# A hybrid mLSTM and attention block on one core: weight blocks split two ahead, and the end of a head in three steps

## Chip, core and metric

The kernel runs on one core of a Trainium2 chip. The metric is the device time of one execution in microseconds (us). The engines are named as in the profile: PE is TensorE, PEld its weight loads, DVE is VectorE, ACT is ScalarE, POOL is GpSimd, SP is SyncE, which here issues most of the DMAs.

## What is computed

One layer over 256 latent tokens and 256 context tokens of width 2048, all in float32. Cut to what matters here:

```python
p   = u @ w_in                       # u: normalised, modulated tokens
h   = mlstm_chunked(q, k, v, ...)    # 8 heads, both directions, dv = 256
h   = rms_norm(h_f + h_b)            # per head
y_a = (sigmoid(o_a) * h * silu(z_a)) @ w_branch_a
y_b = (attention(q_b, k_b, v_b) * silu(z_b)) @ w_branch_b
out = (sigmoid(g_a) * y_a + sigmoid(g_b) * y_b) @ w_out
x   = layer_norm(ALPHA * x + gate * out)
```

o_a, z_a, q_b, z_b, g_a and g_b are columns of p.

## The kernel before

Every large product is made of three matmuls: each float32 operand is split into a high half (rounded to the matmul's float32r) and a low half (what the rounding left), and high x high, high x low and low x high are added up (`three`, lines 335 to 338, and `three_b`, 340 to 343). A weight matrix is read in blocks of 512 KB (`raw`, three buffers, loaded by SP, `fetch_ahead`, line 308). A block is split by two instructions (`split`, 330): ACT casts `raw` to `whi`, then DVE subtracts and writes `wlo`. Two pairs of `whi` and `wlo` lie in one pool; from the second chunk of the second sweep on (`late`, line 722) every third block goes to a third pair. `load_w` (326) is called at the head of a block's products. It first sees to it that LEAD = 2 blocks are split (the one that is about to be used and the next), and then hands out the first.

A product with 256 tokens as output rows (`gemm_tok`, 387) has 8 blocks; in a block there are 4 groups of three matmuls of 512 columns. Before each group it calls `tick`, so a product has 32 ticks, 4 in a block.

Small work is woven into the products. `weave(tasks, 32)` (360) gives a product a list of tasks, and `tick` (348) takes as many as are due, so that they lie evenly over the ticks. A task is a step of a generator: everything up to the next `yield`. The mLSTM heads (`head`, 772) are such generators with HEAD_STEPS = 15 steps, numbered from 0 here:

- step 0 asks SP for the row load of `ws` (783), transposes k on PE (`pk`), scales it on ACT and splits it and v; step 1 splits k and q (`rc`); step 2 is empty.
- steps 3 and 4 make the two context states (`pC`) and split them.
- step 5 (819 to 828) makes the exponents in `ws`, takes exp on ACT and splits the decayed q; step 6 makes the scores `pS` and multiplies them into w; step 7 splits w (840; its low half lies in the tile `rc`); step 8 is empty.
- steps 9 to 12 are the four outputs `ph`: products, a reciprocal on DVE, the scaled sum `hh`, and the square sum.
- step 13 takes the reciprocal root of the square sum (`rsqrt`, 123: an operation on DVE, a power on POOL) and multiplies `hh` by it and by the gate of the head (874). Step 14 transposes `hh` on PE (880) and splits it into the left operand of a later product (`split_to`).

The products that carry the heads are the gate projections. `out_gates(c)` (750) runs for c = 0 to 3 and makes the products o and z, one after the other, each of 8 blocks; after o come two sigmoids on ACT and two multiplies by `mh` on POOL (759), after z two sigmoids on ACT and four multiplies on DVE (766, 767) that complete the gate of heads 2c and 2c + 1. The list `order` (908 to 914) strings the heads together. The last two steps of a head are put among the first of the next head, which so begins before the one ahead of it has ended. `order` is cut into pieces of HEAD_STEPS tasks, one for each o or z product (919); what is left at the end goes, with two empty tasks, to the first product of the attention stage (`group(0)`, q, line 1016).

With 15 tasks on 32 ticks, a piece stands as follows (step at tick; a dash marks the head before or after): 13- at 0, 2 at 3, 3 at 5, 4 at 7, 14- at 9, 5 at 11, 6 at 13, 7 at 15, 8 at 18, 9 at 20, 10 at 22, 11 at 24, 12 at 26, 0+ at 28, 1+ at 30.

The framework that builds the program gives every instruction a priority by its place in the program, allocates tiles from their pools and orders each engine's queue itself; an instruction with all it needs can stand ahead of one that comes before it in the program.

Of the kernel before, what the change touches and what calls it, by code (L numbers as in the profile page):

```python
# [38 lines left out]
LEAD = 2  # L39
# [9 lines left out]
def block_kernel(ctx: ExitStack, tc: tile.TileContext, a: dict, out: bass.AP):  # L49
# [10 lines left out]
    late = []  # L60
    uid = [0]

    def nm(s):
        uid[0] += 1
        return f"{s}_{uid[0]}"
# [14 lines left out]
    def sm(n, w):  # L80
        return tp.tile([P, w], F32, tag=f"sm{w}", name=nm(n), bufs=SMALL[w])
# [41 lines left out]
    def rsqrt(dst, src, scale, eps):  # L123
        w = src.shape[-1]
        t = sm("rs", w)
        nc.vector.tensor_scalar(t, src, scale, eps, op0=ALU.mult, op1=ALU.add)
        nc.gpsimd.tensor_tensor(dst, t, powc[:, :w], op=ALU.pow)
# [107 lines left out]
    def queue(tasks):  # L235

        stream.extend(t[1] for t in tasks if type(t) is tuple)
        return [t[0] if type(t) is tuple else t for t in tasks]
# [69 lines left out]
    def fetch_ahead():  # L308
        while plan and len(early) < DEPTH:
            src, n = plan.pop(0)  # L310
            raw = wp.tile([P, 1024], F32, tag="raw", name=nm("raw"), bufs=3)[:, :n]
            nc.sync.dma_start(raw, src)
            early.append((raw, n))

    def split_ahead(k):
        while len(ready) < k and (plan or early):
            fetch_ahead()
            raw, n = early.pop(0)
            turn[0] += 1
            pool, k_ = (late[0], 1) if late and turn[0] % 3 == 0 else (wp, 2)  # L320
            lo = pool.tile([P, 1024], F32R, tag="wlo", name=nm("wlo"), bufs=k_)[:, :n]
            hi = pool.tile([P, 1024], F32R, tag="whi", name=nm("whi"), bufs=k_)[:, :n]
            split(hi, lo, raw)
            ready.append((hi, lo))

    def load_w():
        split_ahead(LEAD)
        return ready.pop(0)

    def split(hi, lo, src):  # L330

        nc.scalar.copy(hi, src)  # L332
        nc.vector.tensor_tensor(lo, src, hi.bitcast(F32), op=ALU.subtract)  # L333
# [39 lines left out]
    def steps(gen, n):  # L373

        return [lambda: next(gen, None) for _ in range(n)]
# [11 lines left out]
    def gemm_tok(w, n, kts, lhs, toks, tiles):  # L387

        for ks, _, _ in row_blocks(w, n, kts):
            wh, wl = load_w()  # L390
            for b, k in enumerate(ks):
                for i, t in enumerate(toks):
                    tick()
                    need(k)
                    xh, xl = lhs(k, t)
                    three(tiles[i][:, :n], xh, xl, turns(wh[:, b * n:(b + 1) * n]),
                          turns(wl[:, b * n:(b + 1) * n]), k == kts[0], k == kts[-1])

    def gemm_feat(w, kts, regions):


        for ks, _, _ in row_blocks(w, 512, kts):
            wh, wl = load_w()
            for b, k in enumerate(ks):
                for f in range(4):
                    tick()
                    need(k)
                    c0 = b * 512 + f * P
                    for s, o, first, last in regions[f]:
                        us = u[s][k // 4][:, k % 4]  # L410
                        three_b(o, wh[:, c0:c0 + P], wl[:, c0:c0 + P], turns(us[:, 0, :]),
                                turns(us[:, 1, :]), first and k == kts[0], last and k == kts[-1])
# [73 lines left out]
    def prep_tasks(kt):  # L486

        ts = col_tasks(kt) if kt < MOD_PE else unit_tasks((kt, 16 + kt), (0, 1))
        ts.insert(3, lambda: make_x(kt))
        return ts + [lambda: make_u(kt)]  # L490
# [15 lines left out]
    tasks = queue(prep_tasks(0))  # L506
# [126 lines left out]
    def conv(x, hd, n, scale):  # L633

        ac = t2("cva")[:, :n * 256].rearrange("p (s t) -> p s t", s=n)
        sg = t2("cvs")[:, :n * 256].rearrange("p (s t) -> p s t", s=n)
        nc.scalar.activation(ac, x[:, :, 1:257], AF.Identity, bias=cv[:, hd, 3:4], scale=cv[:, hd, 1:2])
        nc.vector.scalar_tensor_tensor(ac, x[:, :, 0:256], cv[:, hd, 0:1], ac, op0=ALU.mult, op1=ALU.add)
        nc.vector.scalar_tensor_tensor(ac, x[:, :, 2:258], cv[:, hd, 2:3], ac, op0=ALU.mult, op1=ALU.add)
        nc.scalar.activation(sg, ac, AF.Sigmoid)  # L640
        nc.vector.scalar_tensor_tensor(x[:, :, 1:257], ac, scale, sg, op0=ALU.mult, op1=ALU.mult)
# [76 lines left out]
    for i in range(18):  # L718
# [7 lines left out]
        fn, _, n = chunks[c]  # L726
# [40 lines left out]
            nc.vector.tensor_tensor(g_[:, t, :], g_[:, t, :], sz, op=ALU.mult)  # L767
        gate_of[c] = g_

    HEAD_STEPS = 15  # L770

    def head(h):
        c, j = h // 2, h % 2
# [96 lines left out]

        rr = sm("rr", 2)
        rsqrt(rr, ss, 1.0 / 256.0, EPS)
        for t in range(2):
            stt(hh[:, t, :], hh[:, t, :], rr[:, t:t + 1], gate_of[c][:, t, j * 256:(j + 1) * 256],
                op0=ALU.mult, op1=ALU.mult)
# [32 lines left out]
    order = []  # L908
    for h in range(8):
        st = steps(head(h), HEAD_STEPS)  # L910
        if h > 0:
            st[2:2], st[6:6] = order[-2:-1], order[-1:]
            order = order[:-2]
        order += st
    n = HEAD_STEPS
    order = [lambda h=h: conv(qT[:, h:h + 1, :], h, 1, 1.0) for h in range(8)] + order
# [96 lines left out]
        half = len(ts) // 2  # L1013
        return ts[:half], ts[half:]

    tasks = order[8 + 7 * n:-1] + [lambda: None] * 2 + order[-1:], []
    for g in range(4):
        tasks = group(g, tasks)

# [191 lines left out]
```

## Time and profile before

| | us |
|---|---|
| median of three runs | 1357.17 |
| lowest and highest run | 1352.03, 1358.71 |
| the profiled execution | 1356.43 |
| its span, first to last instruction | 1354.7 |
| PE busy | 1303.6 |
| DVE busy | 949.0 |
| ACT busy | 650.4 |
| POOL busy | 44.9 |

The profile is of one execution. The span runs from its first instruction to its last; the execution's own time is longer by what lies around it. A row of a timeline gives the start from the span's beginning, the duration, engine, line and instruction, the tiles it writes and reads (out<-in, buffer numbers left out), their shapes, how many instructions were merged into the row, and in brackets how long the engine was idle before it and what ended that. The duration of a matmul holds its passage through the array, so that consecutive matmuls overlap in these rows; their distance from start to start is the pace.

### The profile page before, as it was taken

The page shows a single profiled execution, that of the slowest core. Times are in us where ns is not written, and L with a number is a line of the kernel's source. Part 1 is how long each engine was busy: PE and PEld are TensorE (multiplying, and loading weights), DVE is VectorE, ACT ScalarE, POOL GpSimd, SP SyncE. Part 2 cuts the span into 40 slices and gives each one's busy share as a digit, 9 for nine tenths or more (in the row PEclk, how much of TensorE's full clock was granted, in tenths as well). Part 3 has the DMA queues.
Part 4 walks back from the last instruction along what each step waited for, and adds up shares of the span by engine and source line. Part 5 has one row for each costly group of instructions (what it writes and reads, how often), then busy time and mean ns, then how long its engine had stood idle before and what let it go on. Part 6 is the DMA issues. An engine that isn't in the chain of part 4 may idle for free. (4 is left out here: it accounts for less than half of the span.)

```text
span 1354.7 us, 19750 instructions
## 1 busy us (share of the span) xinstructions
PE 1303.6 (96%) x7613; PEld 1160.6 (86%) x7613; DVE 949.0 (70%) x1537; ACT 650.4 (48%) x929; POOL 44.9 (3%) x74
## 2 busy tenths in 40 slices
PE   5899999999999999999999999999999999999996
PEld 3678889999889988888889999898888888888885
DVE  6589997488745767788778778787555455544657
ACT  3544332154223667766665565666444444444441
POOL 0000000000100000100010000000000000000000
PEclk9999999999999999999999999999999999999998
DMA  8997768535435654445545354434756666576663
GB/s 301 331 326 246 234 210 290 201 124 196 161 110 162 190 193 157 164 167 169 190 148 186 128 169 143 153 125 160 215 200 202 201 195 208 191 281 219 213 219 121
DMA packets 77693, 264.16 MB, mean 195 GB/s; under 512 B 8904, under 2 KB 11608, under 8 KB 76960
## 3 DMA queue, kind: packets, MB, share of 16 engines
q1 hardware_dynamic: 75696, 256.19, 56.3%
q0 software_dynamic: 1296, 6.49, 1.4%
q8 instruction: 59, 0.97, 0.3%
q10 hardware_dynamic: 608, 0.24, 0.1%
q14 instruction: 34, 0.28, 0.1%
HBM read 260.75 MB, written 2.14 MB: 194 GB/s over the span
## 5 line engine op out<-in xcount | busy, mean ns | idle before, releaser
L333 DVE TENSOR_TENSOR wlo<-raw,whi 128x1024 fp32r<-128x1024 f32 (+2 forms) x374 | 444.7, 1192 | 296.0 <-ACT whi L332 295.7
L332 ACT CAST whi<-raw 128x1024 fp32r<-128x1024 f32 (+2 forms) x374 | 379.9, 1019 | 473.9 <-PE p L338 114.9
L336 PE MATMUL p<-whi,u 128*128 128x512 f32 (+1 forms) x448 | 158.7, 361 | 3.7 <-ACT u L298 2.8
L337 PE MATMUL p<-wlo,u 128*128 128x512 f32 (+1 forms) x448 | 159.5, 357 | 2.3 <-DVE wlo L333 2.1
L338 PE MATMUL p<-whi,u 128*128 128x512 f32 (+1 forms) x448 | 157.6, 355 | 0.0
L221 DVE SCALAR_TENSOR_TENSOR junk<-mod,sc 128x1024 bf16<-128x1024 f32 x112 | 134.2, 1219 | 10.0 <-DMA mod<-in_w_mod 9.7
L336 PEld LDWEIGHTS p<-whi,u 128*128 128x128 f32 x448 | 85.2, 192 | 15.5 <-ACT u L298 3.5
L337 PEld LDWEIGHTS p<-wlo,u 128*128 128x128 f32 x448 | 86.0, 192 | 11.2 <-DVE wlo L333 4.1
L338 PEld LDWEIGHTS p<-whi,u 128*128 128x128 f32 x448 | 85.9, 192 | 7.0 <-issue 0.4
L343 PE MATMUL p<-u,wlo 128*128 128x256 f32 x256 | 71.2, 278 | 2.3 <-DVE wlo L333 2.3
L341 PE MATMUL zb<-u,whi 128*128 128x256 f32 x256 | 72.1, 281 | 0.0
L341 PE MATMUL p<-u,whi 128*128 128x256 f32 x256 | 71.1, 278 | 0.0
L342 PE MATMUL p<-u,whi 128*128 128x256 f32 x256 | 70.8, 277 | 0.0
L343 PE MATMUL zb<-u,wlo 128*128 128x256 f32 x256 | 70.4, 275 | 0.0
L342 PE MATMUL zb<-u,whi 128*128 128x256 f32 x256 | 70.4, 275 | 0.0
L337 PE MATMUL z<-wlo,u 128*128 128x512 f32 x128 | 49.2, 384 | 4.3 <-DVE wlo L333 4.3
L337 PE MATMUL o<-wlo,u 128*128 128x512 f32 x128 | 49.1, 383 | 3.5 <-DVE wlo L333 3.4
L343 PEld LDWEIGHTS p<-u,wlo 128*128 128x128 f32 x256 | 49.5, 194 | 3.3 <-DVE wlo L333 2.5
L341 PEld LDWEIGHTS p<-u,whi 128*128 128x128 f32 x256 | 49.4, 193 | 0.4 <-issue 0.4
L336 PE MATMUL q<-whi,u 128*128 128x512 f32 x128 | 49.7, 388 | 0.0
L342 PEld LDWEIGHTS p<-u,whi 128*128 128x128 f32 x256 | 49.5, 193 | 0.0
L336 PE MATMUL ga<-whi,u 128*128 128x512 f32 x128 | 49.4, 386 | 0.0
(330 smaller groups left out, 3145.4 us busy)
## 6 DMA issues: line engine op xcount, KB each, us to landing
mod<-in_w_mod SPq DMA_DIRECT2D x96, 512.0 KB, 5.0
raw<-in_w_g SPq DMA_DIRECT2D x64, 512.0 KB, 4.3
raw<-in_w_o SPq DMA_DIRECT2D x32, 512.0 KB, 4.1
raw<-in_w_z SPq DMA_DIRECT2D x32, 512.0 KB, 4.2
raw<-in_w_qb SPq DMA_DIRECT2D x32, 512.0 KB, 3.9
raw<-in_w_zb SPq DMA_DIRECT2D x32, 512.0 KB, 3.5
raw<-in_w_ba SPq DMA_DIRECT2D x32, 512.0 KB, 3.5
raw<-in_w_bb SPq DMA_DIRECT2D x32, 512.0 KB, 4.1
```

The costliest lines, as they stand in the source:

```text
L221: nc.vector.scalar_tensor_tensor(junk, blk, 1.0, sc[v][:, hf * 1024:(hf + 1) * 1024], op0=ALU.mult, op1=ALU.mult, accum_out=mp[:, v, hf, j ...
L332: nc.scalar.copy(hi, src)
L333: nc.vector.tensor_tensor(lo, src, hi.bitcast(F32), op=ALU.subtract)
L336: mm(o, lhsT=xh, rhs=wh, start=start, stop=False)
L337: mm(o, lhsT=xh, rhs=wl, start=False, stop=False)
L338: mm(o, lhsT=xl, rhs=wh, start=False, stop=stop)
L341: mm(o, lhsT=wh, rhs=xh, start=start, stop=False)
L342: mm(o, lhsT=wh, rhs=xl, start=False, stop=False)
L343: mm(o, lhsT=wl, rhs=xh, start=False, stop=stop)
```

## The change

`load_w` asks for three split blocks instead of two as soon as the third pair exists, so a block is split two blocks ahead of its products. Step 13 of a head is cut in two by a `yield`: 13 is the root, 14 the multiply by the gate, 15 the transposes; a head has 16 steps. The last three steps of a head are put among those of the next at other places: 13 after the next head's step 0, 14 after its step 2, 15 after its step 6. What is left for the first q product gets two empty tasks ahead of step 14 and three ahead of step 15.

```diff
     def load_w():
-        split_ahead(LEAD)
+        split_ahead(3 if late else LEAD)
         return ready.pop(0)
...
-    HEAD_STEPS = 15
+    HEAD_STEPS = 16
...
         rr = sm("rr", 2)
         rsqrt(rr, ss, 1.0 / 256.0, EPS)
+        yield
         for t in range(2):
             stt(hh[:, t, :], hh[:, t, :], rr[:, t:t + 1], gate_of[c][:, t, j * 256:(j + 1) * 256],
...
         if h > 0:
-            st[2:2], st[6:6] = order[-2:-1], order[-1:]
-            order = order[:-2]
+            for at, step in zip((1, 4, 9), order[-3:]):
+                st.insert(at, step)
+            order = order[:-3]
         order += st
...
-    tasks = order[8 + 7 * n:-1] + [lambda: None] * 2 + order[-1:], []
+    tasks = order[8 + 7 * n:-2] + [lambda: None] * 2 + order[-2:-1] + [lambda: None] * 3 + order[-1:], []
```

With 16 tasks on 32 ticks a piece stands as follows, in the numbers of the new steps: 2 at 0, 14- at 2, 3 at 4, 4 at 6, 5 at 8, 6 at 10, 15- at 12, 7 at 14, 8 at 16, 9 at 18, 10 at 20, 11 at 22, 12 at 24, 0+ at 26, 13 at 28, 1+ at 30. The first q product has 21 tasks where it had 17.

## Rows read from the trace of the kernel before

**Rows 1.** The page, busy time of each engine: us, share of the span, instructions.

```profile
PE 1303.6 (96%) x7613; PEld 1160.6 (86%) x7613; DVE 949.0 (70%) x1537; ACT 650.4 (48%) x929; POOL 44.9 (3%) x74
```

**Rows 2.** Busy time in stretches of 100 us: length, then of each engine.

```profile
400.00:500.00 100.00, 99.88 (x691) 94.44 (x690) 64.88 (x90) 51.23 (x69) 3.08 (x3) 1.00 0.55 178
500.00:600.00 100.00, 95.06 (x523) 83.23 (x521) 78.97 (x164) 69.53 (x118) 6.57 (x8) 1.00 0.50 167
600.00:700.00 100.00, 94.72 (x517) 82.57 (x518) 80.89 (x158) 70.10 (x113) 7.76 (x8) 1.00 0.50 165
```

**Rows 3.** What PE waited for, whole span: us in total, times, longest.

```profile
PE z L337 <- DVE wlo L333: 4.3, 6, 1.1
...
PE o L337 <- DVE wlo L333: 3.4, 3, 1.1
...
PE pT L880 <- DVE hh L874: 1.8, 3, 0.7
...
PE q L337 <- DVE wlo L333: 0.4, 1, 0.4
PE ph L338 <- DVE rc L333: 0.2, 1, 0.2
```

**Rows 4.** PE, 565 to 609 us: start, duration, instruction, idle before, releaser.

```profile
573.99 0.38 PE L338 MATMUL o<-whi,u 128*128 128x512 f32 x1
574.21 0.38 PE L336 MATMUL o<-whi,u 128*128 128x512 f32 x1
575.30 0.30 PE L880 MATMUL pT<-cst,hh 128*128 128x128 f32 x1 [0.72 <-DVE hh L874]
576.74 0.48 PE L337 MATMUL o<-wlo,u 128*128 128x512 f32 x1 [1.14 <-DVE wlo L333]
577.06 0.38 PE L338 MATMUL o<-whi,u 128*128 128x512 f32 x1
...
600.08 0.48 PE L337 MATMUL z<-wlo,u 128*128 128x512 f32 x1 [0.37 <-DVE wlo L333]
...
605.39 0.48 PE L337 MATMUL z<-wlo,u 128*128 128x512 f32 x1 [1.11 <-DVE wlo L333]
```

**Rows 5.** ACT, 565 to 607 us, same columns.

```profile
580.27 1.06 ACT L332 CAST whi<-raw 128x1024 fp32r<-128x1024 f32 x1 [1.88 <-DMA raw<-in_w_o]
...
589.91 1.06 ACT L332 CAST whi<-raw 128x1024 fp32r<-128x1024 f32 x1 [2.53 <-PE o L338]
...
592.87 1.28 ACT L823 ACT_TABLE_LOAD   x1
...
597.44 1.06 ACT L332 CAST whi<-raw 128x1024 fp32r<-128x1024 f32 x1
...
602.01 2.00 ACT L332 CAST whi<-raw 128x1024 fp32r<-128x1024 f32 x2
```

**Rows 6.** DVE, 565 to 607 us, same columns.

```profile
574.68 0.87 DVE L874 SCALAR_TENSOR_TENSOR hh<-hh,rr,G 128x256 f32<-128x256 f32 x2
575.47 1.22 DVE L333 TENSOR_TENSOR wlo<-raw,whi 128x1024 fp32r<-128x1024 f32 x1
...
590.32 0.48 DVE L819 SCALAR_TENSOR_TENSOR ws<-ws,gT,cst 128x256 f32<-128x256 f32 x1 [2.37 <-DMA ws<-rows]
...
598.00 0.88 DVE L874 SCALAR_TENSOR_TENSOR hh<-hh,rr,G 128x256 f32<-128x256 f32 x2 [0.91 <-POOL rr L127]
...
603.10 3.37 DVE L333 TENSOR_TENSOR wlo<-raw,whi 128x1024 fp32r<-128x1024 f32 x2 [1.76 <-ACT whi L332]
```

**Rows 7.** POOL, 490 to 720 us, same columns.

```profile
597.25 0.72 POOL L127 TENSOR_TENSOR rr<-rs,powc 128x2 f32<-128x2 f32 x1 [25.17 <-DVE rs L126]
601.72 2.53 POOL L759 TENSOR_TENSOR G<-G,mh 128x512 f32<-128x512 f32 x2 [3.75 <-ACT G L758]
```

**Rows 8.** All engines near the end, 1296 to 1335 us, same columns.

```profile
1299.70 1.05 ACT L332 CAST whi<-raw 128x1024 fp32r<-128x1024 f32 x1 [1.54 <-PE out L338]
...
1302.93 2.34 DVE L333 TENSOR_TENSOR wlo<-raw,whi 128x1024 fp32r<-128x1024 f32 x2
```

## The prediction

> **What bounds the kernel now.** I read the page's busy times first, then the busy time of each stretch, then the list of waits, and last the timelines of one repeat of the stretch where PE waits. PE is busy for 96% of the span [rows 1], so only its pauses can be won. The stretches show where they lie: from 400 to 500 us PE is busy all the time, from 500 to 700 us it lacks 5 us in each 100 [rows 2]. That is the stage in which the gate projections o and z run with the mLSTM heads woven into them, and it is the only place that the change can win from: the start lies ahead of the third buffer pair, and near the end the cast of a block already starts at the moment PE gives a buffer back, two blocks ahead of its use [rows 8].
>
> The waits of that stage are 14: six for a low half of a weight block in z (4.3 us), three in o (3.4), one in the first qb (0.4), three of the closing transposes of a head for the gated hh (1.8), one of a head's products for the low half of w (0.2); together 10.1 us [rows 3]. The idle column is not the whole loss. Two undisturbed matmuls start 0.22 us apart (573.99, 574.21); the transposes start 1.09 after the last one, so their wait costs 0.87 where 0.72 is shown, and the wait for the low half costs 1.44 from start to start, and the matmul after it starts 0.32 later instead of 0.22 [rows 4]. I take 0.27 more for each wait for a weight and 0.15 for one of the transposes: 10.1 + 11 x 0.27 + 3 x 0.15 = 13.5 us. That is the ceiling.
>
> I call the eight weight blocks of a product o0 to o7 and z0 to z7. The late ones are always o2, z1 and z2 (576.74, 600.08, 605.39), once in each of three repeats. From 576.74 to 605.39 lies one product of 32 ticks, so a tick is 0.9 us and a block of four ticks 3.6 [rows 4].
>
> **Why they are late.** ACT works without a pause from 592.87 on: exp of the next head, then its first step, and only at 597.44 the cast of z1; after that the sigmoids of o, and at 602.01 the casts of z2 and z3 [rows 5]. The buffer was not the reason: the cast of z0 got its pair from o5 at 589.91, and o6 gives the next pair back one block later, near 593.5. On DVE the subtraction of z1 comes behind the two gate multiplies of the head before (598.00, 0.88 us), for which DVE had waited 0.91 us on POOL's power; and that of o2 starts at 575.47, behind two such multiplies (574.68) that themselves stand behind the four that make the gate [rows 6]. The engines don't run in the program's order: the first operation of step 5 of the next head (L819) is on DVE at 590.32, some 6 us before the product begins that it is woven into [rows 6]. So the place in the program is a priority among operations that are ready, and this is what the change shifts.
>
> **Part 1, three blocks ready instead of two.** It adds no instruction: the same casts (1.06 us) and subtractions (1.22 us), each placed one block, 3.6 us, earlier in the program. A third buffer pair exists, so a cast placed there waits for the last product of the block before, which has just ended. Behind it on ACT and DVE stand the steps of the head; on SP the load of the block's raw weights is asked for one block earlier, by the same three buffers. Loads are no bound here: one cast of this repeat waited for a load (580.27, 1.88 us), and PE did not wait for that block [rows 4, 5].
>
> **Part 2, the end of a head.** With 16 steps on 32 ticks a step is exactly 2 ticks. Inside the repeat, ticks before and after: the scores pS 13 and 10, the split of w 15 and 14, the outputs ph 20 to 26 and 18 to 24, the next head's first step 28 and 26, the power 32 (tick 0 of the next product) and 28, the gate multiplies 32 and 34, the transposes 41 and 44. The steps hold the same instructions, and no DMA but the row load of step 0, which needs the buffer that the split of w gives back. On POOL the power moves ahead of the gate's two multiplies in the program; in the trace it was already ahead (597.25 against 601.72) [rows 7]. The two steps with nothing in them cost nothing.
>
> **The sum**, three repeats each, by the priorities above:
> Transposes: 0.87 each at most, 2.3 in all. They come 3 ticks (2.7 us) later than now and the multiplies 2 ticks; gone. Alone this would give nothing, since o2's low half ends at 576.69 whatever the transposes do; so it counts only together with the next.
> o2: PE would want it near 574.4 (576.74 less 1.44 and 0.87). The ACT run ahead of it starts with the end of the head, two ticks (1.8 us) earlier; I take 1.3, as that run begins with an exp that waits for a row load and not for a tick. The four multiplies that make the gate still come first; the two of hh no longer do, since o2 is now split at tick 0 and they stand at tick 2 (0.8): 576.69 - 1.3 - 0.8 = 574.6. I keep 0.3 of 1.41: gain 3.3.
> z1: the cast is 1.3 us earlier or more, and POOL's 0.91 no longer stands ahead of the subtraction. The six z waits are 3 x 1.1 for z2 and the rest, 1.0, for z1; with 3 x 0.27 the gain is 1.8.
> z2: its cast comes behind the sigmoids of o in both kernels, so it moves only with the ACT run, 1.3, while PE comes 0.6 earlier through z1. Its subtraction has a second obstacle: the two at 603.10 take 3.37 us, where two undisturbed ones take 2.34 [rows 6, 8], and POOL multiplies the gate from 601.72 to 604.25 [rows 7], so 1.03 us are lost there. If that loss stays, 1.4 - 1.3 + 0.6 = 0.7 of the 1.4 is left; if it goes, nothing. POOL's multiplies follow the same sigmoids and move along, so I keep 0.5 each: gain 2.7. The Trainium skill, page SBUF — State Buffer, section "SBUF: two separate sides", says that VectorE and GpSimd share one pair of ports, held by one instruction for its whole length while the other is blocked; the stretched subtraction agrees. By that rule 0.7 would be left and the sum 0.6 smaller; by the undisturbed duration it would be 1.5 larger.
> qb and ph: 0.6 shown and 0.5 more; the split of w gets 8 ticks from pS to ph instead of 7. Gain 0.5 of 1.1.
> New waits: the last head has 21 steps on the 32 ticks of the first qb instead of 17, so a step is 1.5 ticks instead of 1.9. Not shown in this trace; the nearest rows are the small qb and ph waits (0.2 to 0.4 idle) and the longest wait of the stage, 1.1 [rows 3]. Between nothing and 3 of 1.1 I take 1.0, three small ones, as the last head's chain has the same gap from its step 5 to its outputs (7 ticks) in both.
> Together 2.3 + 3.3 + 1.8 + 2.7 + 0.5 - 1.0 = 9.6 us. The profiled execution took 1356.43 us, its span 1354.7 and 1.7 around it; 1356.4 - 9.6 = 1346.8, told as 1347. The median of the three runs, 1357.17, lies 0.7 above the profiled execution. 0.5% of it, 6.8 us, is about what a measurement of this kernel can tell from no change.
>
> **Rivals.**
> The forecast, any gain from 7 to 13.5: chance 0.60.
> *The priority shifts nothing.* Where ACT is free the casts already run as early as the buffers let them: 589.91 waits 2.53 us for PE to give a buffer back [rows 5]. If the three late ones keep their place behind the head's steps, o2 ends when it does now, the transposes' gain is swallowed by it, and z1 alone wins its 0.91 from POOL: gain 0 to 3, about 1355. For: the whole order is by readiness. Against: the late casts were ready and were passed over. Chance 0.20.
> *POOL decides z2.* The subtraction of z2 can't end before POOL's second gate multiply has (604.25), and if the ACT run begins with the exp at its present time, because the row load lands no earlier, nothing in front of the sigmoids moves: z2 then keeps all of its 1.4 and o2 another 0.7. Gain 9.6 - 2.7 - 3 x 0.7 = 4.8, about 1351.5. This is the port rule of the Trainium skill, page SBUF — State Buffer, taken at its strictest. For: the three z2 subtractions are all stretched. Against: the first step of the next head, a good part of the run, doesn't need the exp. Chance 0.12.
> *Slower: the low half of w.* Step 7 splits w on ACT and DVE, and PE's ph is already waiting for it (0.2 idle, no slack) [rows 3]. If the weight pair that is now placed earlier is taken ahead of that split, each of the eight heads waits for a pair more, 1.06 + 1.22 = 2.28 us, 18.2 in all against the 10.6 won: 1356.4 - 10.6 + 18.2 = 1364. It decides from 1.3 us a head on. Against: in the long run no pair is added, and PE has one tick more there. Chance 0.06.
> That nothing happens because the condition never holds is left out: the third pair is in use in the whole stage. The last 0.02 is for gains beyond the ceiling or mishaps.
>
> **How the numbers follow.** Faster by over 0.5% is below 1350.4: nearly all of the forecast (0.57) and, by the spread of its own terms, some 0.05 of POOL's case: 0.62. Within 0.5%: the rival without a shift (0.20), the rest of POOL's case (0.07) and the edges (0.05): 0.32. Slower by over 0.5%, above 1364: 0.06. The range reaches from the ceiling, 1356.4 - 13.5 = 1343, less 1 for the spread of runs, to 1355 in the rival without a shift: it leaves out the slower case and about half of that rival. The forecast's own range is 1343 to 1350.
>
> **What would show it.** Right: PE busy 98 to 99 us in the stretches 500 to 600 and 600 to 700; no wait of the transposes for hh; z1 and o2 gone from PE's waits or below 0.4; the subtraction of z2 still stretched beside POOL. The cast of z1 near 596 instead of 597.44, measured from the start of z. Wrong: o2 and z1 with the same waits (no shift); ph waiting for the low half of w by over 1 us a head (slower); new waits in qb or zb, where PE has none worth naming now.

## The result, and the profile of the changed kernel

The change makes the kernel slower: the median of seven runs is **1366.42 us** (1361.7 to 1369.06) against 1357.17 of the kernel before, a ratio of 1.0066 with an interval of 1.0047 to 1.0085. That is 9.2 us more where 10 fewer were forecast, and 11 above the upper end of the range. The profiled execution took 1369.06 us, its span 1366.9.

The page's busy times, which answer to [rows 1]:

```profile
PE 1308.1 (96%) x7613; PEld 1160.2 (85%) x7613; DVE 948.4 (69%) x1537; ACT 649.0 (47%) x929; POOL 45.9 (3%) x74
```

The counts are the same and so, within 5 us, is the work. What grew is the time in which PE stands still, and the stretches of 100 us show it in the stage with the heads, which answers to [rows 2]:

```profile
500.00:600.00 100.00, 93.66 (x508) 80.87 (x506) 74.90 (x158) 65.37 (x111) 5.86 (x7) 1.00 0.49 159
600.00:700.00 100.00, 92.13 (x492) 78.51 (x492) 74.55 (x148) 67.82 (x113) 8.48 (x9) 1.00 0.47 156
```

PE is busy for 93.66 and 92.13 us where it was 95.06 and 94.72, and 98 to 99 were to come. The list of PE's waits (us in total, times, longest) answers to [rows 3]:

```profile
PE o L337 <- DVE wlo L333: 5.3, 5, 1.4
PE z L337 <- DVE wlo L333: 4.1, 8, 0.8
...
PE q L337 <- DVE wlo L333: 1.5, 2, 0.8
PE ph L336 <- ACT rb L332: 1.3, 1, 1.3
...
PE ph L338 <- DVE rc L333: 1.1, 2, 0.6
PE ph L337 <- DVE ra L333: 1.0, 1, 1.0
PE pC L338 <- DVE rd L333: 0.7, 3, 0.2
...
PE q L336 <- ACT whi L332: 0.3, 1, 0.3
...
PE z L336 <- ACT whi L332: 0.2, 1, 0.2
```

The transposes no longer wait for hh. But o and z, for which PE waited 9 times, make it wait 14 times now, and the first q and the heads' products more than before: 24 waits and 15.5 us of idle in place of 14 and 10.1. With the 0.27 us that a wait costs beyond its idle time, that is 5.4 + 10 x 0.27 = 8.1 of the 9.2 us. The first matmul of o starts at 462.3 us in both kernels, the first of q at 690.79 instead of 684.01, and the first of zb, the product after q, at 722.39 instead of 713.12: 9.3 us, so the loss is complete there. (The two profiled executions lie 12.6 us apart; the 3 us more come behind that and aren't in the medians.)

**Which blocks.** PE, 599 to 610 us, the head of a z product (start, duration, instruction, idle before, releaser), against [rows 4]:

```profile
599.42 0.38 PE L336 MATMUL z<-whi,u 128*128 128x512 f32 x1
600.37 0.48 PE L337 MATMUL z<-wlo,u 128*128 128x512 f32 x1 [0.57 <-DVE wlo L333]
...
604.70 0.48 PE L337 MATMUL z<-wlo,u 128*128 128x512 f32 x1 [0.21 <-DVE wlo L333]
...
609.02 0.48 PE L337 MATMUL z<-wlo,u 128*128 128x512 f32 x1 [0.79 <-DVE wlo L333]
```

z1 and z2 still come late, and z0, which had never been, is late as well, in two of the three repeats. In the o products it is the same: o2 is late by 0.81, 1.44 and 1.45 us, where it was 1.14 each time, and o0 by 0.78 in two of them. ACT in the same place shows why, against [rows 5]:

```profile
589.24 1.03 ACT L332 CAST whi<-raw 128x1024 fp32r<-128x1024 f32 x1
595.23 1.28 ACT L823 ACT_TABLE_LOAD   x1 [4.95 <-DVE ws L822]
596.52 0.84 ACT L823 ACTIVATE ws<-ws 128x768 f32<-128x768 f32 x1
...
598.02 1.03 ACT L332 CAST whi<-raw 128x1024 fp32r<-128x1024 f32 x1
...
601.58 1.15 ACT L332 CAST whi<-raw 128x1024 fp32r<-128x1024 f32 x1
```

The cast at 589.24 is o7's, the one at 598.02 is z0's. Between them ACT stands idle for 4.95 us in front of the table load and the exp of the next head. Before, z0 was cast at 589.91 and the exp came after it (592.87); now the exp is first. z0 is split into the pair that o5 gives back, and this is o5's last matmul:

```profile
593.13 0.38 PE L338 MATMUL o<-whi,u 128*128 128x512 f32 x1
```

In the kernel before, that matmul started at 589.45 and the cast followed 0.46 us later. So here z0 could have been cast near 593.6; its weights, asked for at 585.74, were there by then, as a block takes 3.4 us here (median of five). ACT was idle until 595.23 and still didn't take it: it went through its queue in order, the load, the exp and some work of the head, and came to z0 at 598.02, 4.4 us late. DVE, against [rows 6], and SP show for what the exp waits:

```profile
586.24 0.94 DVE L333 TENSOR_TENSOR rc<-ws,rb 128x768 fp32r<-128x768 f32 x1
...
592.42 0.48 DVE L819 SCALAR_TENSOR_TENSOR ws<-ws,gT,cst 128x256 f32<-128x256 f32 x1 [3.64 <-DMA ws<-rows]
...
599.09 1.23 DVE L333 TENSOR_TENSOR wlo<-raw,whi 128x1024 fp32r<-128x1024 f32 x1 [0.45 <-ACT whi L332]
...
606.75 3.35 DVE L333 TENSOR_TENSOR wlo<-raw,whi 128x1024 fp32r<-128x1024 f32 x2 [1.34 <-ACT whi L332]
```

```profile
587.21 0.33 SPq L783 DMA_DIRECT2D ws<-rows  x1
```

It is a chain of four: the split of w in the head before gives the buffer of `ws` back (586.24 + 0.94 = 587.18); SP asks for the row load at 587.21; it lands 5.2 us later; at 592.42 step 5 (L819 to L822) begins, and at 595.23 the exp. Both engines stand behind it. The same idle time ahead of the exp is 0.6, 0, 1.6, 0, 1.4, 0, 0.9 us in seven heads of the kernel before, and 5.56, 4.95, 5.25, 5.62, 5.75 in the last five heads of the changed one. The list of DVE's waits, 440 to 760 us, says it in one row, first of the kernel before, then of the changed one:

```profile
DVE ws L819 <- DMA ws<-rows: 10.4, 7, 2.4
```

```profile
DVE ws L819 <- DMA ws<-rows: 22.6, 6, 4.5
```

### The profile page after: what moved, and what is told of

It reads as the page before. It is cut to its first block, busy times and chain, and to the rows that moved or that the text cites. A ratio compares the mean times of both kernels' runs of the same rounds, so it can differ in the third digit from the quotient of the medians.

```text
span 1366.9 us, 19758 instructions
## 1 busy us (share of the span) xinstructions
PE 1308.1 (96%) x7613; PEld 1160.2 (85%) x7613; DVE 948.4 (69%) x1537; ACT 649.0 (47%) x929; POOL 45.9 (3%) x74
## 3 DMA queue, kind: packets, MB, share of 16 engines
q0 software_dynamic: 1296, 6.49, 1.6%
## 4 chain that ended last, share of the span: by engine, by line
PE 41%; DVE 3%; DMA 3%; ACT 2%; issue 1%; DVEq 0%; ACTq 0%
DMA raw<-in_w_out 2%; PE zb L342 2%; PE zb L343 2%; PE zb L341 2%; PE ga L338 2%; PE yb L338 2%; PE ga L336 2%; PE ga L337 2%; PE yb L336 2%; PE yb L337 2%; PE ya L338 2%; PE ya L337 2%; PE ya L336 2%; PE gb L337 2%; PE gb L338 2%; PE gb L336 2%
## 5 line engine op out<-in xcount | busy, mean ns | idle before, releaser
L336 PEld LDWEIGHTS p<-whi,u 128*128 128x128 f32 x448 | 84.8, 190 | 15.5 <-ACT u L298 3.6
L337 PE MATMUL q<-wlo,u 128*128 128x512 f32 x128 | 48.8, 381 | 1.7 <-DVE wlo L333 1.5
```

Of the source, the lines that this page charges most:

```text
L336: mm(o, lhsT=xh, rhs=wh, start=start, stop=False)
L337: mm(o, lhsT=xh, rhs=wl, start=False, stop=False)
```

## The experiments

**Theory A:** the time is lost because the order of ACT and DVE puts step 5 of the next head, which waits for a row load that is asked for late, ahead of casts of weights that are ready. **Theory B:** the casts that part 1 places a block earlier wait for a buffer and hold up what stands behind them. **Theory C:** the new ticks of the head's steps cost PE time by themselves, whatever the queues do. All versions compute the same result. Ratios are to runs of the kernel before in the same round, whose median was 1355.63 to 1357.7, so they don't follow from the first row; "row load" says how step 5 gets its rows: at step 0 into `ws`, as it was; at step 0 into a tile of its own; or at step 2 into `ws`.

| run | steps | blocks ready | row load | median us | ratio, interval |
|---|---|---|---|---|---|
| before | 15 | 2 | step 0 | 1357.17 | 1 |
| changed | 16 | 3 | step 0 | 1366.42 | 1.0066, 1.0047 to 1.0085 |
| e1_lead_only | 15 | 3 | step 0 | 1356.84 | 0.9991, 0.9975 to 1.0007 |
| e2_steps_only | 16 | 2 | step 0 | 1365.07 | 1.0052, 1.0033 to 1.0071 |
| e6_before_rows_apart | 15 | 2 | own tile | 1354.9 | 0.999, 0.9971 to 1.001 |
| e7_lead_rows_apart | 15 | 3 | own tile | 1360.88 | 1.0028, 1.0009 to 1.0047 |
| e8_steps_rows_apart | 16 | 2 | own tile | 1352.01 | 0.9968, 0.9948 to 0.9988 |
| e3_rows_apart | 16 | 3 | own tile | 1354.6 | 0.9973, 0.996 to 0.9987 |
| e13_before_rows_late | 15 | 2 | step 2 | 1351.73 | 0.9968, 0.9948 to 0.9987 |
| e11_lead_rows_late | 15 | 3 | step 2 | 1354.67 | 0.9979, 0.9962 to 0.9996 |
| e12_steps_rows_late | 16 | 2 | step 2 | 1348.09 | 0.9933, 0.9909 to 0.9957 |
| e4_rows_late | 16 | 3 | step 2 | 1349.07 | 0.9949, 0.9928 to 0.997 |
| e10_w_apart | 16 | 3 | step 0, w apart | 1365.63 | 1.0069, 1.0048 to 1.0091 |
| e15_exp_held | 16 | 3 | step 0, step 5 held | 1356.22 | 0.9995, 0.9978 to 1.0013 |

### One part at a time

e1_lead_only is the kernel before with the first hunk of the diff, e2_steps_only the changed kernel without it:

```diff
-        split_ahead(3 if late else LEAD)
+        split_ahead(LEAD)
```

> The changed load_w alone, with the 15 steps of before. Theory A (the exp of the next head stands on ACT's queue ahead of the cast of z0, and waits for its row load, which lands over 5 us after it is asked for): this order has the exp ahead of that cast too, so ACT stands idle some 5 us before the exp in each o and z product, and the time is 1360 to 1368. Theory B (a cast placed two blocks ahead waits for a buffer and holds up what is queued behind it): also 1360 to 1368, but with ACT's idle time before casts, ended by PE. Theory C (the new places of the steps are what costs): no slower than before, 1347 to 1357.

> The 16 steps and their new places alone, with two blocks split ahead as before. Here the cast of z0 stands ahead of the exp, as in the kernel before. Theories A and B: not slower than before, 1349 to 1358, the waits of PE for the transposes gone. Theory C: 1362 to 1369.

Measured: no difference from part 1 alone, and all of the loss from part 2 alone. B falls with e1. My expectation under A fell too, as I had put the misplaced exp down to part 1. In e2 the exp is ahead of the cast in every other product, and ACT idles as long as in the changed kernel (the cast is the first of the next product):

```profile
562.79 1.28 ACT L823 ACT_TABLE_LOAD   x1 [5.59 <-DVE ws L822]
...
566.33 1.09 ACT L332 CAST whi<-raw 128x1024 fp32r<-128x1024 f32 x1
```

DVE's wait for the row load, in the same view as above, is that of the kernel before in e1, and that of the changed kernel in e2:

```profile
DVE ws L819 <- DMA ws<-rows: 9.8, 6, 2.6
```

```profile
DVE ws L819 <- DMA ws<-rows: 22.0, 7, 4.8
```

So it is the steps that bring the exp forward. That e1 gains nothing needs a word of its own. PE's waits in e1:

```profile
PE pC L338 <- DVE rd L333: 3.7, 6, 0.9
PE pC L336 <- ACT rd L332: 3.6, 6, 1.5
...
PE z L337 <- DVE wlo L333: 1.2, 2, 0.8
```

The waits for weights fell as forecast, from 4.3 to 1.2 us in z and from 3.4 to nothing in o [rows 3]. In their place stand twelve waits for the scaled k of the next head, 7.3 us, where there was none. ACT shows its cast, pushed behind the first sigmoid of the gate and its table load:

```profile
598.79 1.28 ACT L758 ACT_TABLE_LOAD   x1
600.08 0.60 ACT L758 ACTIVATE G<-o 128x512 f32<-128x512 f32 x1
600.58 0.61 ACT L332 CAST rd<-kw 128x512 fp32r<-128x512 f32 x1
```

e2 left A, in this revised form, and C standing: both have part 2 to blame, and of the ranges set down for e2 it was C's that held.

### The row load taken out of the way: a tile of its own

If A holds, the changed kernel must win once the rows don't wait for the split of w. e3_rows_apart gives them a tile of their own; e6, e7 and e8 do the same with neither part, with part 1 and with part 2:

```diff
-        pm, pa, w = ws[:, 0:512], ws[:, 512:1024], ws[:, 1024:1792]
-        nc.sync.dma_start(ws[:, 0:1024], G["rows"][h:h + 1, :].broadcast_to([P, 1024]))
+        w = ws[:, 1024:1792]
+        pr_ = t4("pr_")
+        pm, pa = pr_[:, 0:512], pr_[:, 512:1024]
+        nc.sync.dma_start(pr_, G["rows"][h:h + 1, :].broadcast_to([P, 1024]))
```

> The changed kernel, with the row load of a head in a tile of its own, so that it needn't wait until the head before has split w. The work is the same. Theory A: ACT's idle time of 5 us before each exp is gone, and the low halves of z0 and o0 come in time; 1344 to 1354, below both kernels. Theories B and C: the casts wait for the same buffers and the steps stand at the same ticks, so it stays at 1361 to 1368.

> The changed load_w alone with the 15 steps of before, and the row load in a tile of its own. Theory A: 1346 to 1355, well below the changed load_w alone. Theory B: as slow as the changed load_w alone, 1360 to 1368. Theory C: as fast as the changed load_w alone, 1347 to 1357.

> The kernel before with the row load in a tile of its own. Theory A: there the exp hardly waited for its rows, so nothing is won by it, and the loss that the changed load_w alone showed by it (4 us) may return: 1354 to 1363. Theory C: no change, 1354 to 1360.

> The 16 steps alone with the row load in a tile of its own, two blocks split ahead. Theory A: the loss of the steps alone (1365) goes with the wait for the rows: 1349 to 1358. Theory C: it stays, 1362 to 1368.

Measured: the edit is worth 12 us in the changed kernel (1366.42 to 1354.6, which is 0.6 above A's range), 13 in e2's (1365.07 to 1352.01), nothing in the kernel before, and in e1's it costs 4. The 16 steps no longer cost anything (e8 against e6: 2.9 us less, with intervals that overlap). C, with the same ticks, can't explain that. e7 is a miss: PE there waits for `rc` and `rb` of the heads (6.5 and 4.0 us), and why its queues come out so stays open. The tile of its own comes from the pool that also holds the gates, so the edit moves more than one thing.

### The row load asked for later

The opposite edit separates "the load is late" from "its user is queued too early". e4_rows_late asks for the rows two steps later and changes nothing else in the changed kernel:

```diff
-        nc.sync.dma_start(ws[:, 0:1024], G["rows"][h:h + 1, :].broadcast_to([P, 1024]))
...
         split(as_halves(kqh[:, 256:512]), as_halves(kql[:, 256:512]), halves(q))
         yield
+        nc.sync.dma_start(ws[:, 0:1024], G["rows"][h:h + 1, :].broadcast_to([P, 1024]))
         yield
```

> The changed kernel, with the row load asked for two steps LATER (in step 2 instead of step 0). Theory A (revised: with the 16 steps the exp of the next head stands on ACT ahead of the cast of the next product's first block, and its row load lands over 5 us after it is asked for): in this order the exp stands behind the casts of the first three blocks, so although the rows come later, the late first blocks are gone: 1350 to 1360. Theory C (the ticks of the steps themselves): the steps stand where they stood, 1363 to 1369.

Measured: 1349.07, 17 us less than the changed kernel by the medians, 16 by the ratios, from moving one DMA to a later place. DVE's wait for the rows is gone from the list. ACT at the same edge between o and z:

```profile
582.97 1.03 ACT L332 CAST whi<-raw 128x1024 fp32r<-128x1024 f32 x1
...
586.53 1.04 ACT L332 CAST whi<-raw 128x1024 fp32r<-128x1024 f32 x1
...
589.09 1.28 ACT L758 ACT_TABLE_LOAD   x1
...
593.64 1.28 ACT L823 ACT_TABLE_LOAD   x1
```

z begins at 588.46 here. z0 is cast 5.5 us ahead of it (1.4 in the changed kernel) and z1 1.9 ahead (2.2 after), then come the sigmoids and the casts of z2 and z3, and only then the exp. o5's last matmul starts at 582.17 here, so z0 is cast 0.8 us after it, where the changed kernel took 4.9. The rows did not land earlier: SP asks at 585.94, they are there at 590.2, 1.8 us after z began, where the changed kernel had them 7.0 us before. PE's waits in the stage and PE's busy time:

```profile
PE ph L338 <- DVE rb L333: 2.4, 4, 0.8
PE ph L338 <- DVE rc L333: 1.7, 3, 0.7
PE ph L336 <- ACT rb L332: 0.3, 1, 0.3
```

```profile
500.00:600.00 100.00, 98.33 (x542) 86.91 (x541) 84.64 (x164) 75.92 (x124) 10.89 (x10) 1.00 0.51 174
600.00:700.00 100.00, 97.14 (x540) 86.02 (x538) 80.52 (x169) 69.32 (x113) 10.48 (x13) 1.00 0.49 170
```

Not one wait for a weight is left. The stage from the first o to the first q takes 214.1 us, against 221.7 before and 228.5 changed. With one DMA elsewhere, PE is nearly as busy as the prediction had it. How much of the gain is the change's and how much the DMA's, the next runs tell.

The same edit with neither part, with part 1 and with part 2:

> The kernel before with the row load asked for in step 2. If the later request helps only by mending what the change broke, no change: 1354 to 1359. If the exp of the next head, taken early, also stood in the way of the weight casts before the change, o2, z1 and z2 come earlier too: 1348 to 1354, with about the 5 us of ph waits that the changed kernel with late rows shows.

> The changed load_w alone, 15 steps, rows asked for in step 2. If part 1 is worth what was forecast (o2, z1 and z2, some 7 us) once the exp is out of the way, 3 to 7 below the kernel before with late rows; if the later request alone did it, the same as that one within 2.

> The 16 steps alone, two blocks split ahead, rows asked for in step 2. If the new places of the steps cost by themselves, over 1358; if they cost only by the early exp, 1347 to 1354, and 0 to 5 above the whole change with late rows (1349).

Measured, with the row load at step 2 and by the ratios: the edit alone wins 0.32% (e13), part 2 another 0.30 to 0.35% (4 to 5 us: e11 to e4, e13 to e12), and part 1 nothing (e13 to e11, e12 to e4: 0.11 and 0.16% worse, with intervals that overlap), where 3 to 7 us had been expected of it. The intervals of part 2 just overlap too; but of e13 and e12, run in the same round, the slowest run of e12 (1349.17) lies below eleven of the twelve of e13. Neither DVE nor PE waits for the rows in any of the four. The late request also does most of what part 1 was meant for: PE's waits for weights in z, 4.3 us in the kernel before, are 0.3 in e13. In o 3.1 us are left there and nothing in e11, but the heads' products ph wait 6.1 us in e11 instead of 4.1. **e12, 1348.09 us, is the best of all**, 9.6 below the kernel before in its own comparison (1357.7) and so below both kernels.

### Another victim: w in a tile of its own

e10_w_apart leaves the rows in `ws` and takes w out, so that the buffer is free after step 5 and SP can ask for the next rows sooner:

```diff
-        pm, pa, w = ws[:, 0:512], ws[:, 512:1024], ws[:, 1024:1792]
+        pm, pa, w = ws[:, 0:512], ws[:, 512:1024], t4("w")[:, 0:768]
```

> The changed kernel with w in a tile of its own instead, so that the buffer of the rows is free after step 5 and the next row load can be asked for some 8 ticks earlier. Theory A: ACT's idle time before the exp is gone, 1343 to 1354. Theory C: 1362 to 1369.

A miss: 1365.63, as slow as the changed kernel and within C's range. The reason speaks for A all the same. PE hardly waits for weights (1.5 us), but for the low half of w:

```profile
PE ph L338 <- DVE rc L333: 14.7, 6, 4.7
```

DVE at one of the three long ones:

```profile
551.12 0.49 DVE L819 SCALAR_TENSOR_TENSOR w<-ws,gT,cst 128x256 f32<-128x256 f32 x1 [3.64 <-DMA ws<-rows]
...
553.52 0.95 DVE L333 TENSOR_TENSOR rc<-w,rb 128x768 fp32r<-128x768 f32 x1
```

Step 5 of the next head stands ahead of the split of w of the head that is running; its high half had been cast by 548.4 (547.56 + 0.83), and the subtraction waits another 5 us, behind an operation that waits for rows asked for at 545.31. The queue blocks in the same way, with another victim.

### The exp held back, the load left where it is

e15_exp_held is the changed kernel, with the row load at step 0, but step 5 can't be queued ahead of step 3: its column of g is read from a copy that also takes in the context state, times zero, which leaves the values as they are and adds one small DVE operation per head:

```diff
-        g1 = lambda d, t: G["g"][:, d, t, h:h + 1]
+        g1 = lambda d, t: gc[:, d, t:t + 1]
...
+            if d == 0:
+                gc = sm("gc", 4).rearrange("p (d t) -> p d t", d=2)
+                stt(gc, pc[:, 0:4].rearrange("p (d t) -> p d t", d=2), 0.0, G["g"][:, :, :, h],
+                    op0=ALU.mult, op1=ALU.add)
```

> The changed kernel with its row load asked for in step 0 as it is, but with step 5 of a head held back: the column it adds is first copied by an operation that also reads the context state of step 3, so that neither its DVE operations nor the exp can be taken before the product they belong to (8 small DVE operations more). Theory A: it is the place of the exp and of the operations ahead of it, and not when the rows are asked for, that costs: 1347 to 1355, as with late rows, and no idle time of ACT before the exp. If the earlier request of the row load itself hurts (it takes DMA time from the weights), 1362 to 1369 as the change.

Measured: 1356.22, 1.2 us above what A expected. That is 10 of the 17 us between the changed kernel and e4, and all of the 9.2 by which the change was slower. ACT casts z0 at 589.14, and its list has no more idle time ahead of the exp from 500 to 700 us; DVE still waits 10.2 us for the rows, as it did before the change. What is left over are new waits of PE:

```profile
PE ph L336 <- ACT rb L332: 3.9, 4, 1.3
PE ph L338 <- DVE rc L333: 2.1, 4, 0.6
```

The first is for the decayed q, which step 5 makes and which now comes late. So the place of step 5, its DVE operations and the exp, accounts for 10 us with the load untouched. That the row load gets in the way of the weight loads is not what made the change slow: ACT's waits for weights to land, 440 to 760 us, are 19.4 us in the kernel before and 16.8 in the changed one. The other 6 to 7 us to e4 go with the new waits, but no run takes them away one by one.

## Why the prediction was wrong

- **What bounds the kernel, and the ceiling: right.** The pauses of PE in that stage are what could be won; e4 wins 7.6 us of the stage against a ceiling of 13.5 and a forecast of 9.6. But 3.9 of the 7.6 come with the later row load alone (e13), which is no part of the change.
- **Transposes: right, and worth nothing here.** No wait for hh is left in the changed kernel. The prediction says that this counts only together with o2, and o2's idle time went from 3.4 to 3.7 us.
- **The step that failed is in the term for o2, and z1 and z2 rest on it:** "The ACT run ahead of it starts with the end of the head, two ticks (1.8 us) earlier; I take 1.3, as that run begins with an exp that waits for a row load and not for a tick." In the o product of the repeat, before and changed:

```profile
563.45 1.28 ACT L823 ACT_TABLE_LOAD   x1 [1.56 <-DVE r L860]
...
572.61 1.99 ACT L332 CAST whi<-raw 128x1024 fp32r<-128x1024 f32 x2
```

```profile
564.73 1.28 ACT L823 ACT_TABLE_LOAD   x1 [5.56 <-DVE r L862]
...
575.15 2.00 ACT L332 CAST whi<-raw 128x1024 fp32r<-128x1024 f32 x2
```

The first matmul of o is at 567.37 and 568.61, so the run begins 3.9 us ahead of it in both kernels, and not 1.3 earlier. It now holds o0's cast too, and o2's, the first of the last row, comes 6.5 us behind the start of o instead of 5.2: 1.3 later. In the z product the run begins 4.2 us ahead (595.23, 599.42) where it was 3.9 (592.87, 596.74), and holds z0's cast, which had started 3.0 us ahead of it.
- **Under it lies a premise:** "the place in the program is a priority among operations that are ready, and this is what the change shifts". The exp was not ready: it stood at the head of ACT's queue for 5 us. The framework orders the queue when it builds the program, and a late input did not let the next instruction pass: z0's cast could have gone from 593.6 on and went at 598.02. The trace of before had the sign of it: L819 waited 2.37 us for the row load [rows 6], and seven times, 10.4 us, in the whole stage. I read it as a bound on how early the exp could run; it was a sign that the exp was already queued ahead of its data, so that moving it up could only lengthen the wait for whoever stands behind. I put a price on every tick that moved, and none on an order that flips. The rival *POOL decides z2* had the exp at its present time, which is nearly what came; it still gained 4.8 us, as it left z0's cast in its place.
- **z2 and POOL:** the subtraction of z2 is stretched as before (3.35 us for two, 3.37 in [rows 6]), so that rival's obstacle is there, and z2's wait only fell from 1.1 to 0.7 or 0.8 us; it was not what made the kernel slower. By the Trainium skill, page SBUF — State Buffer, section "SBUF: two separate sides", a GpSimd operation that reads SBUF and a VectorE operation with two SBUF inputs exclude each other on their shared ports; the trace agrees as far as the stretch goes, with the two POOL multiplies running from 605.36 to 607.88.
- **New waits in the last head:** 1.0 was taken, with 3.3 as the upper end. In the first q product PE waits 0.33, 0.78, 0.77 and, for `rb`, 1.32 us: 3.2. But the 21 steps are not the cause: e4 has them too, and there the first q product waits for no weight and takes 28.5 us (29.1 before, 31.6 changed). The first two of the four waits are for its first block, as with o0 and z0.
- **The slower rival** had nearly the right time (1364) by luck, and the wrong place: in the changed kernel ph waits 1.1 us for the low half of w. That very wait decides in e10, but the row load causes it, not a weight pair.

Settled by runs: the loss comes with part 2 (e1, e2); it goes when the rows' user no longer holds the queues (e3, e4, e8, e12), and also when only the place of step 5 changes and the load stays where it was (e15). Not settled: why the framework orders it so. That it takes the rows to be there sooner than they are would explain both that it queues step 5 early and that a later request sends it back, but its estimates are not in the trace. Nor is it settled why e7 missed, or what makes up the 6 to 7 us from e15 to e4.

## What to carry to other kernels

Before moving work on an engine that takes its queue in order, as ACT and DVE did here, look for instructions at the head of a queue that wait for a DMA: what stands behind them pays, and a small shift can put an urgent operation there. If such a wait exists, move the request or the operation first (here one DMA line: 17 us in the changed kernel, 0.3% in the one before) and only then judge the change. A buffer that a late step gives back makes the next load late, so follow the chain from the release to the issue, the landing and the first reader before pricing anything by its place in the program.

## What was not expected of the hardware

- A load asked for later made the kernel faster by 17 us. Ten of them are the queue, as e15 wins them with the load untouched; the transfer itself takes 5.5 us (median of seven) in the changed kernel and 4.3 in e4.
- A long pause of PE cost more than its length. In e10, after 4.55 us without work, the next six matmuls of z ran at half the pace (0.42 to 0.43 us from start to start, where 0.22 is usual); the granted clock of the 5 us from 555 on was 0.76, so part of them ran at the lower level, 1.2 GHz. After the other two long pauses (4.66 and 4.34 us) it was 0.66 and 0.69:

```profile
554.52 0.58 PE L338 MATMUL ph<-ra,rc 128*128 128x258 f32 x1 [4.55 <-DVE rc L333]
554.90 0.63 PE L336 MATMUL z<-whi,u 128*128 128x512 f32 x1
```

```profile
555.00:560.00 5.00, 5.00 (x25) 4.30 (x25) 3.39 (x8) 2.26 (x3) 0.00 (x0) 0.76 0.44 162
```

- In e4 the subtractions of z2 and z3 and POOL's multiplies slow each other down on both sides: 3.95 us for the two on DVE (2.34 undisturbed, [rows 8]) and 4.25 for the two on POOL (2.52 in the changed kernel). It costs nothing there, as the blocks are ready in time.
